# An output projection in four units of 1024 columns in place of eight of 512

## The chip, the cores and the metric

The kernel runs on one core of a Trainium2 chip. The metric is device time in microseconds (us), lower is better. The core has engines with a queue of instructions each, which run in the order of that queue and wait for each other through semaphores: PE (matrix products, with PEld loading their stationary operand), DVE (vector), ACT (scalar functions), POOL, and SP, which here only issues DMAs.

## The reference

One layer of a decoder on 256 tokens and 4096 channels, batch 1, all float32. What is computed, cut to what matters here:

```
h = rmsnorm(x, ln_g)
proj = h @ w_in                       # 256x4096 @ 4096x12288
p_x, p_gate, q, k, v, a_gate, s_u, s_gate = split(proj)
y_pool = pool_mixer(p_x)              # 1024 channels
y_attn = stick_breaking_attention(q, k, v)   # 16 heads, 2048 channels
y_ssm  = s5_mixer(s_u)                # 1024 channels, with a 1024x2048 GLU
y_* = rmsnorm(y_*, branch_g) * silu(gate of the branch)
out = rmsnorm(x + concat(y_pool, y_attn, y_ssm) @ w_out, final_g)   # 256x4096 @ 4096x4096
```

## The kernel before

Every large product is done in three passes to keep float32 accuracy: each operand is split into a rounded part `hi` and a rest `lo`, and a product is hi·hi + hi·lo + lo·hi. The activations are split once and stay on the chip as `xhl` (slots of 128 channels, with hi and lo). The weights stream in from memory in 528 pieces ("subs") of 128 partitions x 2 slots x 512 columns (512 KB). For each of them ACT writes `hi` (L232) and DVE writes `lo` (L82, the helper of all two-operand DVE work), and PE then does twelve matmuls of 512 columns: two slots, two halves of the tokens, three passes (L241 to L243). A unit is 512 output columns: 24 units of the input projection with 16 subs each, 4 GLU units with 4 subs, and 8 units of the output projection with 16 subs.

In the output projection five of a unit's sixteen subs (`SEVEN`) are done by Strassen-Winograd: the 2x2 block product of a pair of slots is formed with seven block products of 256 columns in place of eight (L189, `mm_seven`). They need sums of weight blocks (`sums_seven`, tiles `t7` and `sums7`) and of activation blocks (`sums_of_rows`, tiles `s7`), and `join_seven` puts the partial sums together once per unit.

Everything else is side work that hangs on generators, of which `pump(side_q, 3)` takes three steps per sub. The last of it is the gate of the attention branch, `att_gate` (L626): when a unit of kind `ag` has ended, its result is scaled out of PSUM (`agz`, ACT), turned into a sigmoid (`sgm`: ACT three times, DVE, ACT), multiplied with the attention output (`ao`, DVE), transposed by PE (L286, tile `ps_t`) and split into `xhl`. After the fourth `ag` unit the program calls `drain(side_q)` (L905), so this gate is written in full ahead of the first matmul of the output projection. The splits of the other 28 slots of `xhl` are written there as well (L835).

What order the engines see is decided at build time: the scheduler of the framework places PE, ACT and DVE instructions by its own simulation of when their operands are ready; SP's queue keeps the order of the program. PSUM has two pools that stay open to the end: `pmain` (two tiles of 128 x 2 x 512, in turn) for the units, and `pside` for the side work and for the sums of the seven products.

Of the kernel before, what the change touches and what calls it, by code (L numbers as in the profile page):

```python
# [2 lines left out]

# [8 lines left out]
F32 = mybir.dt.float32  # L12
# [19 lines left out]
HELD = 4  # L32
WARM = 8
SUMS_AHEAD = 1
SEVEN = (2, 5, 7, 9, 11)
# [12 lines left out]
    + [("v", V0 + 1024), ("q", Q0 + 1024), ("k", K0 + 1024)]  # L48
    + [("glu", n) for n in (1024, 0, 1536, 512)]
    + [("v", V0 + 1536), ("q", Q0 + 1536), ("k", K0 + 1536)]  # L50
# [3 lines left out]
N_SUB = 24 * 16 + 4 * 4 + 8 * 16  # L54


def body(tc, a, out, ctx):
    nc = tc.nc
    V, S, T = nc.vector, nc.scalar, nc.tensor
# [18 lines left out]
    pm = pool("pmain", space=PSUM)  # L78
    pk = pool("pside", space=PSUM)
# [13 lines left out]
    def act(o, x, f, **kw):  # L93
        S.activation(o, x, f, **kw)  # L94
# [8 lines left out]
    xt0 = bp.tile([P, 2, L], F32, tag="k4", bufs=6, name="xt")  # L103
# [3 lines left out]
    zeros = cp.tile([P, NU], BF16, name="zeros")  # L107
# [22 lines left out]
    held = []  # L130
# [8 lines left out]
    def load(i):  # L139
        w = wp.tile([P, 2, NU], F32, tag="w", bufs=LOAD_AHEAD, name="w")  # L140
        nc.sync.dma_start(w, a["ws"][i])
        wtiles[i] = w

    def hi_lo(dst_hi, dst_lo, src):
        act(dst_hi, src, AF.Copy)
        tt(dst_lo, src, dst_hi.bitcast(F32), ALU.subtract)

    def seven(i):
        return i < N_SUB and subs[i][1] in SEVEN and units[subs[i][0]][0] == "out"

    def sums_seven(i):
        w = wtiles[i]
        left, right = w[:, :, 0:L], w[:, :, L:2 * L]
        t = bp.tile([P, 4, L], F32, tag="k4", bufs=6, name="t7")
        tt(t[:, 0:2, :], right, w[:, 0, :].rearrange("p (c m) -> p c m", c=2), ALU.subtract)
        tt(t[:, 2, :], right[:, 1, :], t[:, 0, :], ALU.subtract)
        tt(t[:, 3, :], left[:, 1, :], t[:, 2, :], ALU.subtract)
        sums = bp.tile([P, 2, 4, L], F32R, tag="k8", bufs=3, name="sums7")
        hi_lo(sums[:, 0], sums[:, 1], t)
        htiles[i] = sums  # L160

    def split_seven(i):
        w = wtiles.pop(i)
        raw = []
        for kk in range(2):
            n = L if kk == 0 else NU
            hi = wp.tile([P, NU], F32R, tag="hi", bufs=5, name="hi")
            lo = wp.tile([P, NU], F32R, tag="lo", bufs=5, name="lo")
            hi_lo(hi[:, 0:n], lo[:, 0:n], w[:, kk, 0:n])
            raw.append((hi, lo))  # L170
        htiles[i] = (raw, htiles[i])

    def mm_seven(i, s, ps, pp):
        (b11, b2), sums = htiles.pop(i)
        xa, xb, y = xhl[:, 2 * s], xhl[:, 2 * s + 1], state["s7"][s]
        lo_half, hi_half = slice(0, P), slice(P, L)
        first = s == SEVEN[0]
        last = s == SEVEN[-1]
        for o, stat, mov, begin, end in (
            (pp[0], xa[:, :, lo_half], [v[:, 0:L] for v in b11], first, last),  # L180
            (ps[:, 0, 0:L], xb[:, :, lo_half], [v[:, 0:L] for v in b2], False, False),
            (ps[:, 0, L:2 * L], y[:, 2], [v[:, L:2 * L] for v in b2], False, False),
            (pp[1], y[:, 0], [sums[:, h, 0] for h in range(2)], False, last),
            (pp[3], xa[:, :, hi_half], [sums[:, h, 1] for h in range(2)], first, last),
            (pp[2], y[:, 1], [sums[:, h, 2] for h in range(2)], False, last),
            (ps[:, 1, 0:L], xb[:, :, hi_half], [sums[:, h, 3] for h in range(2)], False, False),
        ):
            for k, (p, q) in enumerate(((0, 0), (0, 1), (1, 0))):
                T.matmul(o, stat[:, p, :], mov[q], start=begin and k == 0, stop=end and k == 2, skip_group_check=True)  # L189

    def join_seven(pp, xr):
        e = bp.tile([P, 4, L], F32, tag="k4", bufs=6, name="e7")
        act(e[:, 0, :], pp[0], AF.Copy)
        tt(e[:, 3, :], e[:, 0, :], pp[2], ALU.add)
        tt(e[:, 1, :], e[:, 3, :], pp[1], ALU.add)
        tt(e[:, 2, :], e[:, 3, :], pp[3], ALU.add)
        tt(e[:, 3, :], e[:, 2, :], pp[1], ALU.add)
        tt(xr, xr, e.rearrange("p (t c) m -> p t (c m)", t=2), ALU.add)

    def sums_of_rows(qp, srcs):  # L200
        state["s7"] = {}
        for s in SEVEN:
            xa, xb = srcs(2 * s), srcs(2 * s + 1)
            t = qp.tile([P, 3, P], F32, tag="t", bufs=1, name="ts")
            tt(t[:, 0, :], xa[:, P:L], xb[:, P:L], ALU.add)
            tt(t[:, 1, :], t[:, 0, :], xa[:, 0:P], ALU.subtract)
            tt(t[:, 2, :], xb[:, 0:P], t[:, 1, :], ALU.subtract)
            tt(xa[:, P:L], xa[:, 0:P], xa[:, P:L], ALU.subtract)
            y = qp.tile([P, 3, 2, P], F32R, name="s7_%d" % s)
            hi_lo(y[:, :, 0, :], y[:, :, 1, :], t)  # L210
            state["s7"][s] = y
            yield

    def split(i):
        if seven(i):
            return split_seven(i)
        w = wtiles.pop(i)
        for kk in range(2):
            if i < KT // 2:
                split_x(2 * i + kk)  # L220
            h = 2 * (i - N_SUB + HELD) + kk
            if h < 0:
                hi = wp.tile([P, NU], F32R, tag="hi", bufs=5, name="hi")
                lo = wp.tile([P, NU], F32R, tag="lo", bufs=5, name="lo")
            elif h < 6:
                if h % 2 == 0:
                    held.append(bp.tile([P, 2, 2, NU], F32R, tag="k8", bufs=3, name="held8"))
                hi, lo = held[-1][:, kk, 0, :], held[-1][:, kk, 1, :]
            else:
                held.append(bp.tile([P, 2, NU], F32R, tag="k4", bufs=6, name="held4"))  # L230
                hi, lo = held[-1][:, 0, :], held[-1][:, 1, :]
            made = S.activation(hi, w[:, kk, :], AF.Copy)  # L232
            if i == 12:
                state["gate"] = made.ins.name
            tt(lo, w[:, kk, :], hi.bitcast(F32), ALU.subtract)
            htiles[i, kk] = (hi, lo)

    def mm_tok(ps, stat, slot, hi, lo, first, last, toks=(0, 1)):
        for t in toks:
            sl = slice(t * P, t * P + P)  # L240
            T.matmul(ps[t], stat[:, slot, 0, sl], hi, start=first, stop=False)  # L241
            T.matmul(ps[t], stat[:, slot, 0, sl], lo, start=False, stop=False)  # L242
            T.matmul(ps[t], stat[:, slot, 1, sl], hi, start=False, stop=last)  # L243


    state = {}
# [3 lines left out]
    def load_x(piece):  # L250
        xt = bp.tile([P, 2, L], F32, tag="k4", bufs=6, name="xt")
        nc.sync.dma_start(xt, a["xT"][piece])
        xtiles[piece] = xt
# [6 lines left out]
    def square_x(piece):  # L260
        xr = bp.tile([P, 2, NU], F32, tag="k4", bufs=6, name="xsq")
        nc.sync.dma_start(xr, a["xr"][piece])
        square_sums(x_sums, xr, piece)
# [17 lines left out]
    def transposed(y, kts, emit):  # L281
        for h in range(2):
# [4 lines left out]
            for c in range(2):  # L287
                emit(kts[h * 2 + c], ps[:, c * L:c * L + L])
            yield

    def keep(dst):
        def emit(kt, ps):
            act(dst(kt), ps, AF.Copy, scale=branch_g[:, kt:kt + 1])
        return emit

    def direct(kt, ps):
        slot = OUT_KT.index(kt)
        g = branch_g[:, kt:kt + 1]
        act(xhl[:, slot, 0, :], ps, AF.Copy, scale=g)
        stt(xhl[:, slot, 1, :], ps, g, xhl[:, slot, 0, :].bitcast(F32), ALU.mult, ALU.subtract)  # L300

    def square_sums(dst, y, n):
        junk = bp.tile([P, 512], BF16, tag="junk", bufs=1, name="junk")
# [20 lines left out]
    def pool_unit(u, px):  # L324
        yp = bp.tile([P, 2, NU], F32, tag="k4", bufs=6, name="ypool")
# [27 lines left out]
    ypT = bp.tile([P, 8, L], F32, tag="k8", bufs=3, name="ypT")  # L353

    def pool_gate(u, z):
        sg = bp.tile([P, 2, NU], F32, tag="k4", bufs=6, name="sgm")
# [7 lines left out]
        yield from transposed(y, [4 * u + c for c in range(4)], keep(lambda kt: ypT[:, kt, :]))  # L364


    uT = bp.tile([P, 8, L], F32, tag="k8", bufs=3, name="uT")
    glu = {}
# [109 lines left out]
    def ssm(sp, wait_u):  # L478
# [11 lines left out]
        for ct in range(8):  # L490
# [13 lines left out]
            for half in range(2):  # L504
# [13 lines left out]
                for j in range(2):  # L518
                    r0 = 32 * (2 * half + j)
                    for b in range(3):  # L520
                        side_dma(u3[32 * b:32 * b + 32, j, :], uT[r0:r0 + 32, ct, :])
# [45 lines left out]
            stt(y, uT[:, ct, :], d_skip[:, ct:ct + 1], ps[:, 0:L], ALU.mult, ALU.add)  # L567
# [4 lines left out]
            tt(uT[:, ct, :], y, l, ALU.mult)  # L572
# [6 lines left out]
    def attention(lp, g, vt, qt, kt):  # L579
        ao = lp.tile([P, 2, NU], F32, name="ao%d" % g)  # L580
        aout[g] = ao
# [41 lines left out]
        square_sums(att_sums, ao, g)  # L623
        yield
# [406 lines left out]
```

## Time and profile before

| What | us |
|---|---|
| median of 3 runs (1537.27 to 1538.69) | 1537.94 |
| the execution that was profiled, its time | 1538.15 |
| its span in the trace | 1536.4 |
| outside the span (1538.15 less 1536.4) | 1.75 |
| mean granted clock of PE | 0.998 |

The profile is one execution. A page of it gives busy times by engine, the chain of work that ended last and the costliest groups; further views give the waits, the single instructions in order of time, and busy times by stretch of the span. Times in them are counted from the start of the span. A matmul is pipelined: its row lasts longer than the step to the next one, so what a matmul costs is read from the starts of neighbours.

### The profile page before, as it was taken

Reading aid. Unit: us, or ns where it says so; the run is one execution under the profiler, and the core shown is the slowest. Engines: PE = TensorE matmul, PEld = TensorE weight load, DVE = VectorE, ACT = ScalarE, POOL = GpSimd, SP = SyncE. Lnnn points to the kernel's source line nnn. Section 1 sums busy time; section 2 is a strip of 40 time slices with the busy share of each in tenths; the row PEclk is TensorE's granted clock in tenths of the full one; section 3 lists DMA queues with packets and bytes.
Section 4 is the critical chain, followed back from the end, with each engine's and each line's share of the span. In section 5 each row is a group of like instructions: output and inputs, shape, how many; then the busy total and the mean of one; then the engine's idle time right before and its main releaser. Section 6 shows DMA issues by size and latency. Waiting matters only on the chain.

```text
span 1536.4 us, 21621 instructions
## 1 busy us (share of the span) xinstructions
PE 1521.1 (99%) x7328; PEld 1266.3 (82%) x7328; DVE 1186.9 (77%) x2304; ACT 931.6 (61%) x1677; POOL 0.2 (0%) x4
## 2 busy tenths in 40 slices
PE   9999999999999999999999999999999999999996
PEld 7888788878788888788888888888888888888885
DVE  7579878999899879897645744555677988888886
ACT  7765556766566655575546755456677655555554
POOL 0000000000000000000000000000000000000000
PEclk9999999999999999999999999999999999999999
DMA  9866655665656556554655555555655666666665
GB/s 336 310 220 202 194 179 187 196 209 185 209 187 196 189 165 200 189 179 159 191 192 178 182 185 189 192 164 178 192 183 187 218 221 213 223 210 206 216 215 199
DMA packets 94351, 308.22 MB, mean 201 GB/s; under 512 B 11808, under 2 KB 17696, under 8 KB 94240
## 3 DMA queue, kind: packets, MB, share of 16 engines
q1 hardware_dynamic: 84096, 295.92, 58.5%
q10 hardware_dynamic: 10144, 10.92, 2.5%
q8 instruction: 57, 0.93, 0.3%
q14 instruction: 54, 0.44, 0.1%
HBM read 299.45 MB, written 4.19 MB: 198 GB/s over the span
## 4 chain that ended last, share of the span: by engine, by line
PE 96%; DVE 2%; DMA 1%; ACT 0%; issue 0%; SPq 0%; DVEq 0%; ACTq 0%
PE pm L242 29%; PE pm L241 28%; PE pm L243 28%; PE ps L189 3%; PE pm L189 2%; DMA w<-in_ws 1%; PE ps_y L562 1%; PE ps_c L658 1%; DVE lo L82 1%; PE ps_bu L535 1%; PE ps_z L588 0%; PE ps_p L346 0%; PE ps_t L286 0%; DVE t L82 0%; PE ps_z L606 0%; DVE sums L82 0%
## 5 line engine op out<-in xcount | busy, mean ns | idle before, releaser
L82 DVE TENSOR_TENSOR lo<-w,hi 128x512 fp32r<-128x512 f32 (+1 forms) x1048 | 697.5, 680 | 272.5 <-ACT hi L232 266.3
L232 ACT ACTIVATE hi<-w 128x512 fp32r<-128x512 f32 x968 | 602.3, 629 | 455.0 <-PE pm L243 270.0
L242 PE MATMUL pm<-lo,xhl 128*128 128x512 f32 x1872 | 732.7, 391 | 0.2 <-DVE lo L82 0.2
L241 PE MATMUL pm<-hi,xhl 128*128 128x512 f32 x1872 | 730.9, 391 | 1.1 <-ACT xhl L94 0.6
L243 PE MATMUL pm<-hi,xhl 128*128 128x512 f32 x1872 | 731.0, 391 | 0.0
L241 PEld LDWEIGHTS pm<-hi,xhl 128*128 128x128 f32 x1872 | 351.8, 188 | 75.1 <-ACT hi L232 1.7
L242 PEld LDWEIGHTS pm<-lo,xhl 128*128 128x128 f32 x1872 | 351.8, 188 | 74.4 <-issue 2.9
L243 PEld LDWEIGHTS pm<-hi,xhl 128*128 128x128 f32 x1872 | 351.8, 188 | 71.2 <-issue 0.8
L91 DVE SCALAR_TENSOR_TENSOR et<-et,pw,tr 128x16 f32<-128x16 f32 (+3 forms) x256 | 56.2, 277 | 1.5 <-ACT tr L94 1.3
L94 ACT ACTIVATE sums<-t 128x1024 fp32r<-128x1024 f32 x40 | 42.3, 1057 | 24.6 <-DVE t L82 24.6
L82 DVE TENSOR_TENSOR sums<-t,sums 128x1024 fp32r<-128x1024 f32 x40 | 48.9, 1223 | 9.2 <-ACT sums L94 9.2
L94 ACT ACTIVATE hi<-w 128x256 fp32r<-128x256 f32 x80 | 40.0, 518 | 23.4 <-PE pm L243 19.7
L94 ACT ACTIVATE tr<-et,pw 128x32 f32<-128x32 f32 (+3 forms) x128 | 45.4, 386 | 9.6 <-DVE et L91 5.5
L189 PE MATMUL ps<-sums,s 128*128 128x256 f32 x240 | 46.8, 285 | 0.9 <-DVE sums L82 0.9
L82 DVE TENSOR_TENSOR t<-w 128x512 f32<-128x512 f32 x40 | 27.6, 690 | 22.0 <-DMA w<-in_ws 21.9
L550 DVE TENSOR_TENSOR_SCAN tb<-rho,ta 128x256 f32<-128x256 f32 x64 | 40.7, 680 | 0.1
L189 PEld LDWEIGHTS ps<-sums,s 128*128 128x128 f32 x240 | 36.7, 192 | 1.7 <-DVE sums L82 1.5
L82 DVE TENSOR_TENSOR t<-w,t 128x256 f32<-128x256 f32 x80 | 33.7, 421 | 0.3
L94 ACT ACTIVATE sgm<-sgm 128x1024 f32<-128x1024 f32 x24 | 25.3, 1052 | 0.2
L243 PE MATMUL pm<-hi,hhl 128*128 128x512 f32 x64 | 25.3, 395 | 0.0
L242 PE MATMUL pm<-lo,hhl 128*128 128x512 f32 x64 | 25.2, 393 | 0.0
L241 PE MATMUL pm<-hi,hhl 128*128 128x512 f32 x64 | 25.1, 392 | 0.0
(259 smaller groups left out, 1123.7 us busy)
## 6 DMA issues: line engine op xcount, KB each, us to landing
w<-in_ws SPq DMA_DIRECT2D x527, 512.0 KB, 3.4
xsq<-in_xr SPq DMA_DIRECT2D x8, 512.0 KB, 6.5
xr<-in_xr SPq DMA_DIRECT2D x8, 512.0 KB, 4.5
xt<-in_xT SPq DMA_DIRECT2D x15, 256.0 KB, 6.0
b<-in_bst ACTq DMA_DIRECT2D x16, 192.0 KB, 3.8
u<-uT ACTq DMA_DIRECT2D x96, 32.0 KB, 2.6
out<-o SPq DMA_DIRECT2D x6, 512.0 KB, 4.1
fg<-in_fg SPq DMA_DIRECT2D x8, 256.0 KB, 5.5
```

The costliest lines, as they stand in the source:

```text
L82: V.tensor_tensor(o, x, y, op)
L91: V.scalar_tensor_tensor(o, x, s, y, op0, op1)
L94: S.activation(o, x, f, **kw)
L189: T.matmul(o, stat[:, p, :], mov[q], start=begin and k == 0, stop=end and k == 2, skip_group_check=True)
L232: made = S.activation(hi, w[:, kk, :], AF.Copy)
L241: T.matmul(ps[t], stat[:, slot, 0, sl], hi, start=first, stop=False)
L242: T.matmul(ps[t], stat[:, slot, 0, sl], lo, start=False, stop=False)
L243: T.matmul(ps[t], stat[:, slot, 1, sl], hi, start=False, stop=last)
L535: T.matmul(ps[:, c, :], b3r[:, j, c, :], u3r[:, j, :], start=c == 0, stop=True, skip_group_check=True)
L550: V.tensor_tensor_scan(tb[:, c, :], rho[:, pr:pr + 1].broadcast_to([P, L]), ta[:, c, :], 0.0, ALU.mult, ALU.add)
L562: T.matmul(ps[32 * j:32 * j + 32, 0:L], cf[:, j, c, :], ss[j][:, c, :], start=c == 0, stop=c == 1, skip_group_check=True)
L658: T.transpose(ps[:, (c * 2 + t) * P:(c * 2 + t + 1) * P], z[:, t, (h * 2 + c) * P:(h * 2 + c + 1) * P], ident)
```

## The change

- The output projection has four units of 1024 columns. A unit still has 16 pairs of slots, but each pair comes as two subs (h = 0 and 1, one for each half of the columns, laid out so by the host).
- Six of 16 pairs are done with seven products, and a block has 512 columns. Both subs of a pair are split together (`split_seven`): four differences of 512 columns, then splits of 1024, 512, 1024 and 1024 columns.
- All other splits are of 1024 columns in one instruction per engine (before: two of 512). Rings of `hi` and `lo` hold four such splits, six in the output projection. Weight loads run six subs ahead there; for the first three units two of six land in the part of `o` that the fourth will fill.
- PSUM: the two pools are closed at the start of the output projection, and one of four tiles of two banks each is opened, of which a unit has two for its result and two for the sums of the seven products, in turn with the next unit.
- The transposed branch outputs go to DRAM (`kept`, queue of POOL), and come back during the last `ag` unit (`take_back`, queue of SP), where they are split into `xhl` four slots at a time with the row sums of their pair. So do the attention outputs (`kept_a`, read back as `ya`) and the gate of the S5 branch. `mm_tok` takes both slots for one half of the tokens before the other.
- The GLU units stand after the last v, q and k units.

What the scheduler makes of it is shown at three places. First PE's queue around the end of the last `ag` unit. Before, with `pm_11691` the tile of the first output unit, `ao3` the gated attention output, `ps_7` and `s7` of the seven products:

```order
L189 MATMUL pm_11691<-hi_11776,xhl_97 128x256
L189 MATMUL ps_7_11697<-lo_11773,xhl_97 128x256
L189 MATMUL ps_7_11697<-hi_11772,xhl_97 128x256
L189 MATMUL ps_7_11697<-sums7_11724,s7_5_11185 128x256 x3
L189 MATMUL ps_7_11697<-sums7_11724,xhl_97 128x256 x3
L189 MATMUL ps_7_11697<-sums7_11724,s7_5_11185 128x256 x3
L286 MATMUL ps_t_11663<-ident_75,ao3_9974 128x128 x4
L286 MATMUL ps_t_11672<-ident_75,ao3_9974 128x128 x4
L189 MATMUL pm_11691<-lo_11777,xhl_97 128x256
```

Now, with `pm_9715` the tile of the last `ag` unit, `pm_10130` that of the first output unit, and `ya` the gated attention output:

```order
L260 MATMUL pm_9715<-lo_10025,xhl_102 128x512
L261 MATMUL pm_9715<-hi_10024,xhl_102 128x512
L259 MATMUL pm_9715<-hi_10024,xhl_102 128x512
L260 MATMUL pm_9715<-lo_10025,xhl_102 128x512
L261 MATMUL pm_9715<-hi_10024,xhl_102 128x512
L304 MATMUL ps_t_10102<-ident_80,ya_10091 128x128 x4
L304 MATMUL ps_t_10111<-ident_80,ya_10091 128x128 x4
L259 MATMUL pm_10130<-hi_10042,xhl_102 128x512
L260 MATMUL pm_10130<-lo_10043,xhl_102 128x512
```

Before, the transposes of the last gate stood in the middle of the sixth pair of the first output unit; now they stand between the last matmul of the `ag` unit and the first of the output projection.

Second, DVE's queue from the last `agz` to the product that these transposes read. Before, the piece around the end of the gate:

```order
L91 SCALAR_TENSOR_TENSOR sgm_11654<-agz_11595,sgm_11654 128x1024
L82 TENSOR_TENSOR lo_11742<-w_11681,hi_11741 128x512
L82 TENSOR_TENSOR lo_11746<-w_11681,hi_11745 128x512
L82 TENSOR_TENSOR sums7_11724<-t7_11720,sums7_11724 128x1024
L82 TENSOR_TENSOR lo_11773<-w_11710,hi_11772 128x256
L82 TENSOR_TENSOR t7_11780<-w_11770 128x512
L82 TENSOR_TENSOR ao3_9974<-ao3_9974,sgm_11654 128x1024
```

Now (`yk` are the blocks that `take_back` brings, `ts` and `y7` their row sums, `o` the region in which a weight piece landed); ahead of this piece stand nine more rows that follow the `hi` that ACT makes between the two `agz`:

```order
L101 SCALAR_TENSOR_TENSOR sgm_10093<-agz_10088,sgm_10093 128x1024
L92 TENSOR_TENSOR ts_10048<-ts_10048,yk_10046 128x128
L92 TENSOR_TENSOR yk_10046<-yk_10046 128x128
L92 TENSOR_TENSOR t7_10176<-o_10126 128x512 x2
L92 TENSOR_TENSOR ts_10048<-yk_10046,ts_10048 128x128
L92 TENSOR_TENSOR t7_10177<-o_10126,t7_10176 128x512
L92 TENSOR_TENSOR xhl_102<-yk_10046,xhl_102 128x4x256
L101 SCALAR_TENSOR_TENSOR ya_10091<-ya_10091,r_b2048_9047,agz_10088 128x512 x2
L92 TENSOR_TENSOR t7_10177<-o_10126,t7_10177 128x512
L92 TENSOR_TENSOR lo_10185<-t7_10176,hi_10184 128x1024
L92 TENSOR_TENSOR y7_12_10052<-ts_10048,y7_12_10052 128x3x128
L92 TENSOR_TENSOR ya_10091<-ya_10091,sgm_10093 128x1024
```

The row sums and splits of the last two `yk` and the weight sums of the first seven-product pair now stand between the sigmoid and the product, ahead of the transposes.

Third, ACT's queue in the same place, now:

```order
L104 ACTIVATE agz_10088<-pm_9714,rtok_86 128x512
L104 ACTIVATE hi_10140<-w_10040 128x1024
L104 ACTIVATE agz_10088<-pm_9715,rtok_86 128x512
L104 ACTIVATE hi_10158<-w_10070 128x1024
L104 ACTIVATE sgm_10093<-agz_10088 128x1024
L104 ACTIVATE xhl_102<-yk_9998 128x4x256
L104 ACTIVATE sgm_10093<-sgm_10093 128x1024
L104 ACTIVATE y7_10_10004<-ts_10000 128x3x128
L104 ACTIVATE sgm_10093<-sgm_10093 128x1024 x2
```

Before, splits of 512 and 256 columns stood between the same steps:

```order
L94 ACTIVATE agz_11595<-pm_11206,rtok_81 128x512 x2
L94 ACTIVATE hi_11683<-w_11544 128x256
L94 ACTIVATE hi_11687<-w_11544 128x512
L94 ACTIVATE sgm_11654<-agz_11595 128x1024
L232 ACTIVATE hi_11712<-w_11573 128x512
L94 ACTIVATE sgm_11654<-sgm_11654 128x1024
```

The core of the diff:

```diff
-SEVEN = (2, 5, 7, 9, 11)
+SEVEN = (2, 4, 6, 8, 10, 12)
...
     def split_seven(i):
...
+        b, a = flat(wtiles.pop(i)), flat(wtiles.pop(i + 1))
+        b11, b21, b12, b22 = b[:, 0:NU], b[:, NU:], a[:, 0:NU], a[:, NU:]
...
+        tt(t0, b12, b11, ALU.subtract)
+        tt(t1, b22, b12, ALU.subtract)
+        raw, one, low, high = ring(), ring(), ring(), ring()
+        hi_lo(*raw, b)
+        tt(t2, b22, t0, ALU.subtract)
+        tt(t3, b21, t2, ALU.subtract)
+        hi_lo(one[0][:, 0:NU], one[1][:, 0:NU], b22)
+        hi_lo(*low, t[0])
+        hi_lo(*high, t[1])
...
+    def take_back(g):
+        t = bp.tile([P, 4, L], F32, tag="k4", bufs=K4, name="yk")
+        nc.sync.dma_start(t, kept[g])
+        for h in range(2):
+            s = 2 * g + h
+            if s in SEVEN:
+                row_sums(state["out_rows"], state["s7_out"], s, t[:, 2 * h, :], t[:, 2 * h + 1, :])
+                row_difference(t[:, 2 * h, :])
+        hi_lo(xhl[:, 4 * g:4 * g + 4, 0, :], xhl[:, 4 * g:4 * g + 4, 1, :], t)
...
     def start_end():
         nonlocal ep
         drain(side_q)
         late_ctx.close()
+        psum_ctx.close()
         ep = end_ctx.enter_context(tc.tile_pool(name="end", bufs=1, side="right", reuse_waits="tile"))
         state["o"] = ep.tile([P, 2, D], F32, name="o")
...
+        state["po"] = end_ctx.enter_context(tc.tile_pool(name="pout", bufs=1, space=PSUM, reuse_waits="tile"))
...
-            side_q.append(att_gate(lp, n, z))
-            if n == 3:
-                for i in range(28):
-                    hi_lo(xhl[:, i, 0, :], xhl[:, i, 1, :], y_src(i))
+            side_q.append(att_gate(n, z))
...
+        if kind == "ag" and c == A_G + 1536 and s >= 2 and s % 2 == 0:
+            take_back(s // 2 - 1)
...
+            mm_tok(into, rows, (2 * s, 2 * s + 1), pair, s == 0, s == nk // 2 - 1, (0,) if late else (0, 1))
...
+    sums = cp.tile([P, 2, 2], F32, name="last_sums")
     for t in range(2):
+        for h in range(2):
...
+            tt(last[:, t, cols], ps[t][:, h, :], last[:, t, cols], ALU.add)
+            act(state["joined"][t][:, h, :], last[:, t, cols], AF.Square, accum_out=sums[:, t, h:h + 1])
+        tt(out_sums[:, t, 3:4], sums[:, t, 0:1], sums[:, t, 1:2], ALU.add)
```

More of the change, by code (lines that the diff above doesn't have):

```diff
@@ L144, in hi_lo @@
     def hi_lo(dst_hi, dst_lo, src):
-        act(dst_hi, src, AF.Copy)
+        made = act(dst_hi, src, AF.Copy)
         tt(dst_lo, src, dst_hi.bitcast(F32), ALU.subtract)
-    def seven(i):
[L149 to L160, printed above, removed]
@@ new lines, in split @@
+    def split(i):
+        if i < KT // 2:
+            split_x(2 * i)
+            split_x(2 * i + 1)
+        if seven(i):
+            if subs[i][2] == 0:
+                split_seven(i)
+            return
+        w = flat(wtiles.pop(i))
+        raw = ring()
+        for n in (slice(0, NU), slice(NU, WIDE)) if i < 3 else (slice(0, WIDE),):
+            made = hi_lo(raw[0][:, n], raw[1][:, n], w[:, n])
+        if i == 12:
+            state["gate"] = made.ins.name
+        htiles[i] = raw
@@ L214, in split @@
[L214 to L236, printed above, removed]
@@ L687, in body @@
         units.append((kind, c, 8 if kind == "glu" else KT))
[L688 removed]
+    for n in range(4):
         units.append(("out", n, KT))
@@ L692, in body @@
         for s in range(nk // 2):
-            subs.append((ui, s))
+            for h in range(2 if kind == "out" else 1):
+                subs.append((ui, s, h))
     assert len(subs) == N_SUB
@@ L853, in body @@
     delayed = []
-    for i, (ui, s) in enumerate(subs):
+    for i, (ui, s, h) in enumerate(subs):
         kind, c, nk = units[ui]
```

392 lines of the change are left out of this document (203 added, 189 removed).

## The prediction

> **What bounds the kernel now.** I read the page first: how busy the engines are, and which of them the chain that ended last runs through.
>
> ```profile
> span 1536.4 us, 21621 instructions
> PE 1521.1 (99%) x7328; PEld 1266.3 (82%) x7328; DVE 1186.9 (77%) x2304; ACT 931.6 (61%) x1677; POOL 0.2 (0%) x4
> ...
> PE 96%; DVE 2%; DMA 1%; ACT 0%; issue 0%; SPq 0%; DVEq 0%; ACTq 0%
> ```
>
> PE is the bound: 96% of the chain is PE following PE. Busy PE need not be PE at its pace, so I look at PE's own waits next (engine and line, what it waited for, us in total, times, longest).
>
> ```profile
> PE ps_i L111 <- DVE zeros L108: 1.2, 1, 1.2
> PE ps L189 <- DVE sums L82: 0.9, 2, 0.5
> PE pm L241 <- DVE o L82: 0.8, 1, 0.8
> ...
> PE pm L241 <- ACT hi L232: 0.5, 1, 0.5
> ```
>
> Hardly anything: some 4 us in 1536. So time can be won only with fewer or shorter matmul steps, and is lost wherever PE is made to wait. What is a step? The timeline of PE in a quiet stretch (start, duration) gives that of 512 columns, the chain in order of time (start, length) that of 256.
>
> ```profile
> 399.82 0.39 PE L242 MATMUL pm<-lo,xhl 128*128 128x512 f32 x1
> ...
> 410.02 0.39 PE L242 MATMUL pm<-lo,xhl 128*128 128x512 f32 x1
> ```
>
> ```profile
> 1212.10 0.96 PE ps L189 x8
> ```
>
> These are the first and last of 46 rows: 45 steps in 10.20 us, 0.2267 each. Eight matmuls of 256 columns take 0.96, 0.120 each: two of them cost 0.240, six per cent more than one of 512.
>
> **Term 1, fewer and wider products: −8.3 us.** Before, a unit has 11 pairs of 12 matmuls of 512 columns and 5 pairs of 21 of 256; eight units make 1056 and 840, so 1056 x 0.2267 + 840 x 0.120 = 340.2 us. Now a unit has 10 pairs of 24 and 6 of 21, all of 512 columns; four units make 1464, and 331.9 us. The other units keep their matmuls, the side work its 456.
>
> The Trainium skill's "TensorE: Matmul & The Clock Gate", section Back-to-back issue gap, gives a warm step as the columns over 2.4 GHz plus 2.5 ns: an estimate by it is 215.8 and 109.2 ns, and a saving of 3.7 us in place of 8.3. This trace has 226.7 and 120 ns, and it decides.
>
> **Term 2, the border of input and output projection: +16 us.** The last gate's transposes are now in PE's queue ahead of the first output matmul (first place shown above). They read the product of `ya` and the sigmoid, which starts from the result of the very matmuls that end just before. Before, the same gate ran as follows (timeline of all engines; start, duration, what):
>
> ```profile
> 1179.91 1.27 ACT L94 ACTIVATE agz<-pm,rtok 128x512 f32<-128x512 f32 x2 [0.15 <-PE pm L243]
> ...
> 1181.02 1.41 DVE L91 SCALAR_TENSOR_TENSOR ao<-ao,r_b,agz 128x512 f32<-128x512 f32 x2
> ...
> 1181.90 1.05 ACT L94 ACTIVATE sgm<-agz 128x1024 f32<-128x1024 f32 x1
> ...
> 1183.37 1.06 ACT L94 ACTIVATE sgm<-sgm 128x1024 f32<-128x1024 f32 x1
> ...
> 1184.84 1.05 ACT L94 ACTIVATE sgm<-sgm 128x1024 f32<-128x1024 f32 x1
> ...
> 1188.08 1.22 DVE L91 SCALAR_TENSOR_TENSOR sgm<-agz,sgm 128x1024 f32<-128x1024 f32 x1
> ...
> 1189.47 1.04 ACT L94 ACTIVATE sgm<-sgm 128x1024 f32<-128x1024 f32 x1
> ...
> 1192.48 1.23 DVE L82 TENSOR_TENSOR ao<-ao,sgm 128x1024 f32<-128x1024 f32 x1
> ...
> 1194.71 0.49 PE L286 MATMUL ps_t<-ident,ao 128*128 128x128 f32 x3
> ```
>
> From the scaling to the transposes are 14.8 us, and PE spent them on output matmuls. In the new queue it has none that it may take. For the new length I go through DVE's queue, the later of the two, with these rows (count, busy, mean ns):
>
> ```profile
> L82 DVE TENSOR_TENSOR lo<-w,hi 128x512 fp32r<-128x512 f32 x1008 | 683.2, 690 | 272.3 <-ACT hi L232 266.3 <-ACT hi L94 0.5 <-DMA w<-in_ws 0.3
> L82 DVE TENSOR_TENSOR sums<-t,sums 128x1024 fp32r<-128x1024 f32 x40 | 48.9, 1223 | 9.2 <-ACT sums L94 9.2
> L94 ACT ACTIVATE sums<-t 128x1024 fp32r<-128x1024 f32 x40 | 42.3, 1057 | 24.6 <-DVE t L82 24.6
> ...
> L82 DVE TENSOR_TENSOR cf<-ta,tb 128x128 f32<-128x128 f32 x8 | 2.3, 287 | 0.0
> ...
> L82 DVE TENSOR_TENSOR s<-ts,s 128x384 fp32r<-128x384 f32 x5 | 2.8, 552 | 0.0
> ```
>
> Let zero be the end of the last `ag` matmul. The last five matmuls are of the other half of the tokens, so the first `agz` starts at −1.1; with 0.69 for it and 1.06 for the `hi` behind it, DVE gets its first row of this stretch at 0.65. From there to the product stand 23 rows: seven of 1024 columns (8.6), eight of 128 (2.3), two of 384 (1.1), four of 512 (2.8), and the two multiplications of `ya` (0.75 each by the row at 1181.02): 16.3 us. Neighbours overlap by some 0.09 (that row has two in 1.41), which takes off 2.0; and DVE waits some 1.1 in all for ACT, whose rows of 1.06 (sigmoid, two `yk`) come in the order shown. 0.65 + 16.3 − 2.0 + 1.1 is 16.0, which I take; 14.8 of the old one, with other rows between, is near. The bounds: the dependent steps alone are 0.69 + 4 x 1.05 + 2 x 1.22 = 7.3; with neither overlap nor early rows it is 18. While PE stands, DVE and ACT run on: four output subs (10.9 us of PE) and the sums of the first seven-product pair are then ready, so no second wait follows.
>
> **Term 3, the clock after it: +1.7 us.** A window behind PE's last work and a later one (us from and to, busy times, then PEclk), and the first matmuls of the span:
>
> ```profile
> 1525.30:1530.40 5.10, 0.00 (x0) 0.00 (x0) 3.64 (x10) 2.89 (x6) 0.00 (x0) 1.00 0.77 302
> 1530.70:1536.00 5.30, 0.00 (x0) 0.00 (x0) 0.00 (x0) 0.00 (x0) 0.00 (x0) 0.50 0.81 317
> ```
>
> ```profile
> 1.18 3.59 PE L111 MATMUL ps_i<-zeros 128*128 128x512 bf16 x8 [1.18 <-DVE zeros L108]
> ```
>
> The granted clock falls to 0.50 some 5 us after PE stops, and the first eight matmuls of 512 columns step by 0.427 (3.59 less a last one of 0.6, over 7) instead of 0.2267. A stall of 16 us passes the five. If the return takes as long as that start, 3.6 us, 8.4 steps lose 0.20 each: 1.7. Bounds 0 and 3.4 (twice as long).
>
> **Term 4, small waits that go: −0.9 us**, the wait for `sums` above: operands are ready six splits ahead now. Bounds −2 and +4: by the rows above a seven-product pair costs DVE 4 x 0.69 + 3 x 1.22 + 0.69 = 7.1 us and a plain one 2.4, a unit with join and end (4 x 0.69 + 6 x 1.22) 77 us against 83 of PE. In a window in the middle of the output projection it was 41.69 of 50:
>
> ```profile
> 1350.00:1400.00 50.00, 50.00 (x271) 43.43 (x270) 41.69 (x68) 29.27 (x52) 0.00 (x0) 1.00 0.62 207
> ```
>
> So DVE goes from 83% to 93%, still behind PE.
>
> **Term 5, the end: +0.4 us.** Before, the second half of the tokens waited for the read of the first:
>
> ```profile
> 1518.79 0.69 DVE L82 TENSOR_TENSOR o<-pm,xr 128x512 f32<-128x512 f32 x1 [1.06 <-PE pm L243]
> 1519.52 0.63 ACT L94 ACTIVATE xr<-o 128x512 f32<-128x512 f32 x1 [4.88 <-DVE o L82]
> 1519.54 0.50 PE L241 MATMUL pm<-held,xhl 128*128 128x512 f32 x1 [0.78 <-DVE o L82]
> ```
>
> Now the halves lie in tiles of their own and that 0.8 goes. But the second quarter of the last half waits for the read of the first quarter, which stands on DVE behind two additions (0.69 each), the second square on ACT (0.63) and three short rows: some 1.4. Then come an extra short addition, and one wide product (1.22) as last work where two of 512 stood. I take +0.4 (−0.8 to +1.5).
>
> **At nothing:** the wide splits of the input projection (1.22 on DVE for 1.38; a sub has 2.72 us of PE), the GLU units' new place, and the DMAs that move. Behind the seven `yk` loads on SP stand weight loads that are up to four subs, 10.9 us of PE, early; 512 KB landed in 3.4 us in the median:
>
> ```profile
> w<-in_ws SPq DMA_DIRECT2D x527, 512.0 KB, 3.4
> ```
>
> Uncovered, a late one would cost 1 or 2 us. The row sums of `take_back` fill DVE's gaps in the last `ag` unit: per two subs some 2.9 + 2.4 us against 5.44 of PE.
>
> **Sum:** the profiled execution's 1538.15 (0.21 above the median) − 8.3 + 16 + 1.7 − 0.9 + 0.4 = **1547.0 us**, 0.6% slower. What can be told from no change is about 0.2%, 3.1 us.
>
> **The rivals.**
>
> - *The gate is ready in time (faster, 1529).* If PE passed the waiting transposes, or the product stood before the last `ag` matmul ends, terms 2 and 3 fall away: 1538.15 − 8.3 − 0.9 + 0.4 = 1529.3. It decides at a stall of about 8.8 us, where term 1 is eaten up. For it: the build's scheduler took this order. Against it: the product's first operand is the `ag` result, and in the row at 1519.54 PE stood until what it waited for had come. The skill's page on TensorE calls PE's queue a partial reorder window of 64 entries that pulls weight loads ahead, and in the section The mechanism has matmuls strictly in order; by the first alone one could hope for 1529, by the second not. Chance 0.07.
> - *A short stall (same, 1537).* If DVE and ACT had done the `yk` and `t7` rows before the end of the unit, only the dependent 7.3 us would be left, too short or nearly so to touch the clock after: 1538.15 − 8.3 + 7.3 − 0.9 + 0.4 = 1536.7. Against it: these rows stand behind waits for the end of the unit. Chance 0.07.
> - *DVE takes over in the output projection (1556 or more).* At 93% any wait of DVE for a weight piece counts: the `t7` rows, which need both pieces of a pair, waited 22 us in 40 before:
>
> ```profile
> L82 DVE TENSOR_TENSOR t<-w 128x512 f32<-128x512 f32 x40 | 27.6, 690 | 22.0 <-DMA w<-in_ws 21.9
> ```
>
> At 0.55 each, 24 pairs would add 13 us to 4 x 77, still under 332; it takes 1 us per pair to pass PE, and then each further 0.4 us per pair costs 9: 1556. Chance 0.11.
>
> **How the numbers follow.** Forecast 0.75: its own range, with a stall of 10 to 18 us and the bounds of the other terms, is 1539 to 1553. The range is to leave out no more than the first rival and some of the others: 1538 to 1555. Slower: 0.75 + 0.11 = 0.86; same 0.07; faster 0.07.
>
> **What would show it.** PE's waits should list one of about 16 us for DVE `ya` at the transposes, followed by steps of 0.43 us and a dip of PEclk in the slice at 1180 us. From there to the last matmul it should be some 332 us plus the eight transposes, with steps of 0.227. If no such wait is there, term 2 is wrong and the time is near 1529; if waits for `lo` or `t7` are spread over the output units, the third rival holds.

## The result, and the profile after

| What | us |
|---|---|
| changed kernel, median of 4 runs (1548.92 to 1552.07) | 1550.53 |
| kernel before, median of 4 runs (1537.27 to 1539.75) | 1538.32 |
| ratio, 95% interval | 1.0079 (1.0061 to 1.0096) |
| profiled execution of the changed kernel, its time | 1550.40 |
| its span (before: 1536.4) | 1548.6 |

The change makes the kernel slower by 0.8%. In a later job the same kernel took 1549.06 against 1537.16 of the kernel before, ratio 1.0077 (1.0064 to 1.0091).

First the page: busy times by engine, and the row of the granted clock over the span in 40 slices.

```profile
span 1548.6 us, 19301 instructions
PE 1517.0 (98%) x6896; PEld 1243.1 (80%) x6896; DVE 1148.9 (74%) x1729; ACT 854.0 (55%) x1118; POOL 10.5 (1%) x23
...
PE   9999999999999999999999999999995999999996
...
PEclk9999999999999999999999999999998999999998
```

PE is busy for 4.1 us less than before (1517.0 against 1521.1) in a span that is 12.2 longer. One slice, the 31st, has PE at 5 tenths and the clock at 8: there the time is. PE's waits name it (engine and line, what it waited for, us in total, times, longest):

```profile
PE ps_t L304 <- DVE ya L92: 15.9, 1, 15.9
PE ps_i L121 <- DVE zeros L118: 1.2, 1, 1.2
PE pm L259 <- ACT hi L104: 0.9, 1, 0.9
PE pm L259 <- DVE o L92: 0.8, 1, 0.8
PE pm L259 <- DVE gl L92: 0.7, 1, 0.7
```

The first row is new; the one for `sums` of before is gone. The timeline of PE at the border of input and output projection (start, duration):

```profile
1180.80 0.39 PE L261 MATMUL pm<-hi,xhl 128*128 128x512 f32 x1
1197.06 1.94 PE L304 MATMUL ps_t<-ident,ya 128*128 128x128 f32 x8 [15.87 <-DVE ya L92]
1198.66 0.78 PE L259 MATMUL pm<-hi,xhl 128*128 128x512 f32 x1
1199.23 0.63 PE L260 MATMUL pm<-lo,xhl 128*128 128x512 f32 x1
1199.66 0.63 PE L261 MATMUL pm<-hi,xhl 128*128 128x512 f32 x1
...
1202.22 0.48 PE L261 MATMUL pm<-hi,xhl 128*128 128x512 f32 x1
1202.53 0.39 PE L259 MATMUL pm<-hi,xhl 128*128 128x512 f32 x1
1202.76 0.39 PE L260 MATMUL pm<-lo,xhl 128*128 128x512 f32 x1
```

The wait ends with the transposes, which then take 1.60 us to the next start; after them the starts lie 0.43 apart, and from 1202.53 on 0.227 again. In the 16 us before, DVE's and ACT's rows were these (parts of it):

```profile
1181.63 0.68 ACT L104 ACTIVATE agz<-pm,rtok 128x512 f32<-128x512 f32 x1
...
1187.48 1.22 DVE L101 SCALAR_TENSOR_TENSOR sgm<-agz,sgm 128x1024 f32<-128x1024 f32 x1
...
1189.02 1.29 DVE L92 TENSOR_TENSOR t<-o 128x512 f32<-128x512 f32 x2
...
1191.03 1.22 DVE L92 TENSOR_TENSOR xhl<-yk,xhl 128x1024 fp32r<-128x1024 f32 x1
...
1192.17 1.41 DVE L101 SCALAR_TENSOR_TENSOR ya<-ya,r_b,agz 128x512 f32<-128x512 f32 x2
...
1195.70 1.22 DVE L92 TENSOR_TENSOR ya<-ya,sgm 128x1024 f32<-128x1024 f32 x1
```

The product of the last row is what PE waits for. Between it and the sigmoid's row at 1187.48 DVE works through rows that belong to other things (`t`, `xhl<-yk`). Last, windows over the same stretch (from and to, its length, busy times of PE, PEld, DVE, ACT and POOL, then the granted clock):

```profile
1183.00:1185.00 2.00, 0.00 (x0) 0.00 (x0) 1.97 (x5) 2.00 (x3) 0.00 (x0) 1.00 1.02 408
1185.00:1187.00 2.00, 0.00 (x0) 0.00 (x0) 1.75 (x3) 2.00 (x4) 0.00 (x0) 0.58 1.03 412
1187.00:1189.00 2.00, 0.00 (x0) 0.00 (x0) 1.90 (x5) 0.71 (x2) 0.00 (x0) 0.50 0.87 346
...
1199.00:1202.40 3.40, 3.40 (x10) 2.63 (x9) 3.03 (x7) 1.34 (x3) 0.00 (x0) 0.50 0.02 5
1202.40:1206.00 3.60, 3.60 (x18) 2.96 (x17) 1.23 (x1) 1.06 (x1) 0.00 (x0) 1.00 0.00 0
```

PE stopped at 1181.03 (its last start plus one step). A window of 2 us at a mean of 0.58 that goes from 1.00 to 0.50 turns at 1185.3, 4.3 us after the stop; the clock is back at 1202.4, 5.3 us after the first transpose.

### The profile page after: what moved, and what is told of

It is laid out like the page before. It is cut to its first block, busy times and chain, and to the rows that moved or that the text cites. A ratio compares the mean times of both kernels' runs of the same rounds, so it can differ in the third digit from the quotient of the medians.

```text
span 1548.6 us, 19301 instructions
## 1 busy us (share of the span) xinstructions
PE 1517.0 (98%) x6896; PEld 1243.1 (80%) x6896; DVE 1148.9 (74%) x1729; ACT 854.0 (55%) x1118; POOL 10.5 (1%) x23
## 4 chain that ended last, share of the span: by engine, by line
PE 97%; DVE 1%; ACT 1%; DMA 0%; issue 0%; SPq 0%; DVEq 0%
PE pm L259 28%; PE pm L260 28%; PE pm L261 28%; PE p L227 4%; PE pm L227 3%; PE ps_y L599 1%; PE ps_c L693 1%; PE ps_t L304 1%; PE ps_bu L572 0%; PE ps_p L381 0%; PE ps_z L624 0%; DMA w<-in_ws 0%; PE ps_z L642 0%; PE ps_p L373 0%; PE ps_av L654 0%
## 5 line engine op out<-in xcount | busy, mean ns | idle before, releaser
L92 DVE TENSOR_TENSOR lo<-w,hi 128x1024 fp32r<-128x1024 f32 (+1 forms) x499 | 595.2, 1197 | 315.3 <-ACT hi L104 313.2
L104 ACT ACTIVATE hi<-w 128x1024 fp32r<-128x1024 f32 (+1 forms) x499 | 515.9, 1038 | 489.7 <-PE pm L261 452.0
L261 PE MATMUL pm<-hi,xhl 128*128 128x512 f32 x1856 | 725.2, 391 | 0.0
L259 PE MATMUL pm<-hi,xhl 128*128 128x512 f32 x1856 | 719.7, 391 | 2.4 <-ACT hi L104 0.9
L104 ACT ACTIVATE hi<-t 128x1024 fp32r<-128x1024 f32 x48 | 50.9, 1061 | 25.4 <-ACT hi L104 7.5
L92 DVE TENSOR_TENSOR lo<-t,hi 128x1024 fp32r<-128x1024 f32 x48 | 58.3, 1221 | 4.9 <-ACT hi L104 4.7
L104 ACT ACTIVATE hi<-o 128x1024 fp32r<-128x1024 f32 (+1 forms) x32 | 30.7, 978 | 32.5 <-PE pm L261 30.6
L92 DVE TENSOR_TENSOR lo<-o,hi 128x1024 fp32r<-128x1024 f32 (+1 forms) x32 | 35.4, 1122 | 12.0 <-ACT hi L104 11.7
L227 PE MATMUL p<-hi,y 128*128 128x512 f32 x96 | 37.6, 391 | 0.0
L227 PE MATMUL pm<-hi,xhl 128*128 128x512 f32 x96 | 37.6, 391 | 0.0
L227 PE MATMUL p<-hi,xhl 128*128 128x512 f32 x96 | 37.6, 391 | 0.0
```

The lines of the kernel that those rows point to most:

```text
L92: V.tensor_tensor(o, x, y, op)
L104: return S.activation(o, x, f, **kw)
L227: T.matmul(o, stat[:, p, :], pair[q][:, n], start=start and k == 0, stop=stop and k == 2, skip_group_check=True)
L259: T.matmul(ps[t], stat[:, slot, 0, sl], hi[:, n], start=begin, stop=False, skip_group_check=True)
L261: T.matmul(ps[t], stat[:, slot, 1, sl], hi[:, n], start=False, stop=end, skip_group_check=True)
```

## The experiments

Theory A: the change loses its gain at the border, where PE waits 15.9 us for the last gate and then runs at half clock; the output projection itself is faster, and bound by PE. Rivals: the wait costs little by itself, DVE is the bound behind it, or the wait is set by something else than DVE's queue.

**The wait alone, in the kernel before** (e3). The first output matmuls get an order dependency on the gate's transposes; nothing else changes.

```diff
-            T.matmul(ps[t], stat[:, slot, 0, sl], hi, start=first, stop=False)
+            d = T.matmul(ps[t], stat[:, slot, 0, sl], hi, start=first, stop=False)
+            if state.get("border"):
+                tc.add_manual_dep(d.ins, state["turned"], ...)
```

> The kernel before with one thing added: the first output matmuls stand behind the last gate's transposes on PE, as in the change. Theory A: PE waits from the end of the ag unit to the product, up to the 14 us that the gate took before, less where DVE and ACT get there sooner because their rings of splits are full; then half clock for some 5 us (2.6 us): slower than before by 12 to 17, 1550 to 1555. Rival B (the wait is mostly taken up again, since the splits run ahead and the waits of the output projection go): slower by less than 6, under 1544.

Measured: 1547.42, ratio 1.0059 (1.0042 to 1.0076), slower by 9.2 and short of the 12 expected. PE's timeline says why:

```profile
1180.02 0.39 PE L249 MATMUL pm<-hi,xhl 128*128 128x512 f32 x1
1182.84 0.58 PE L189 MATMUL ps<-hi,xhl 128*128 128x256 f32 x1 [2.44 <-ACT hi L94]
...
1186.26 0.84 PE L189 MATMUL ps<-sums,s 128*128 128x256 f32 x3
1191.25 1.94 PE L292 MATMUL ps_t<-ident,ao 128*128 128x128 f32 x8 [4.15 <-DVE ao L82]
1192.84 0.78 PE L241 MATMUL pm<-hi,xhl 128*128 128x512 f32 x1
```

The scheduler moved twelve products of 256 columns, which my dependency did not cover, into the gap, and the gate's product came 10.9 us after the unit's end in place of 14.0. What is left of waiting up to the transposes, 11.0 us behind the unit's end, is 9.6, the half clock is there again (starts 0.43 apart), and some small waits later go. So an old kernel with nothing of the change but the order at the border loses most of what the change loses. The rival (under 6) falls.

**Without the wait, in the changed kernel** (e1 and e2). e1 moves the seven-product pairs by two, so that their PSUM tile is free at first; e2 also leaves the last gate's transposes for the first output unit, in that tile.

```diff
-SEVEN = (2, 4, 6, 8, 10, 12)
+SEVEN = (4, 6, 8, 10, 12, 13)
```

```diff
+            if state["out"]:
+                ps = state["p7"][:, h, :]
+            else:
                 ps = pk.tile([P, 512], F32, tag="ps", bufs=2, name="ps_t")
...
+            if n == 3:
+                pump(side_q, 2)
+                state["last"] = side_q.popleft()
...
             start_end()
+            side_q.append(state["last"])
```

> The changed kernel with the seven-product pairs at 4, 6, 8, 10, 12, 13 instead of 2, 4, 6, 8, 10, 12 (still six of 16); it is also the control of e2 and e7. Theory A (PE waits at the border for the product of ya, and DVE's queue sets when that comes): the four differences of weight blocks and one of their splits (4 x 0.69 + 1.22, overlapping, 3.9 us in the trace of the change) no longer stand between the sigmoid and the product, a plain split of 1.22 does; from the trace's end of the sigmoid on DVE at 1188.7 the remaining rows take 4.4, the product ends near 1194.2 instead of 1196.9, so the wait is 13.3 us instead of 15.9 and the time 1548. Rival B (ACT's chain sets the product, DVE only fills gaps): the wait stays 15.9 and the time 1550.5.

Measured for e1: 1551.13, ratio 1.0085 (1.0070 to 1.0100). The wait for `ya` is 14.1, 1.8 shorter than in the change: DVE's rows between sigmoid and product count, though not for all of the 2.6 that I gave them. The time did not follow: the profiled execution is only 0.7 shorter than that of the change (spans 1547.9 and 1548.6), and the median is no lower. By the starts of PE the transposes begin some 2 earlier, but the end of the kernel gives back 1.5: the last wait for `o` grew from 0.8 to 1.3, and from the last matmul to the end of the span it is 12.8 us in place of 11.7. With a seven-product pair at 13, the rows that join the sums stand on DVE right before the last additions.

> e1 with the last gate's transposes put into the first output unit: they go through the PSUM tile that the unit's seven products use from pair 4 on, so PE has output matmuls to take first. Theory A (the border costs the wait of 15.9 us and 2.8 us of half clock behind it, and nothing else of the change costs as much): no long wait, no dip of the clock, 1550.5 - 15.9 - 2.8 = 1531.8, faster than before by 6.5. Rival B (DVE is short of time there: in the 16 us of the wait it was busy 14; without the wait the first output subs wait for their splits instead): waits for lo or t7 in the first eight subs of 3 us or more, 1535 or more.

Measured for e2: 1535.71, ratio 0.9984 (0.9975 to 0.9993): 15.4 us under e1, and faster than the kernel before. The long wait and the dip of the clock are gone, but 3.9 are missing from the 18.7 of theory A. PE's waits, and windows behind the border, of e2:

```profile
PE pm L260 <- DVE lo L92: 1.5, 1, 1.5
...
PE pm L259 <- DVE o L92: 0.8, 1, 0.8
```

```profile
1196.00:1201.00 5.00, 5.00 (x25) 4.12 (x25) 5.00 (x7) 0.29 (x1) 0.00 (x0) 1.00 0.61 209
1201.00:1206.00 5.00, 5.00 (x24) 4.02 (x23) 5.00 (x11) 4.14 (x7) 0.00 (x0) 1.00 0.29 110
1206.00:1211.00 5.00, 3.40 (x17) 2.19 (x15) 5.00 (x7) 2.73 (x3) 0.00 (x0) 1.00 0.47 154
```

DVE (third engine of a row) is busy without a gap for 15 us, and PE has to wait for a `lo`: rival B is right in part, with a smaller wait than its 3 us. The rows that DVE did while PE stood must still be done, and now they stand beside output matmuls. Another part of what is missing is the end, which e2 has from e1: 12.6 us behind the last matmul in place of 11.7.

**DVE in the first output unit** (e9, e12). e9 gives unit 0 only the pairs 6, 8, 10, 12. Its pairs 2 and 4 then take activation blocks whose second half has been replaced by the difference that seven products need, so unit 0 computes something else than the reference; the work of all engines is that of plain pairs.

```diff
-        return units[ui][0] == "out" and s in SEVEN
+        return units[ui][0] == "out" and s in (SEVEN if units[ui][1] else SEVEN_0)
```

> e2 with the pairs of the change (2, 4, 6, 8, 10, 12) in the output units 1 to 3 and four pairs (6, 8, 10, 12) in unit 0. In e2 PE waited 2 us for one lo at the end of pair 4's products while DVE was busy without a gap from 1196 to 1211. Theory B' (with the wait at the border gone, DVE is short in the first output unit, and that is where part of the gain went): two pairs less in unit 0 free 9 us of DVE there, the 2 us go, and 2 x 3 matmuls more cost 1.4: 1535.7 - 2.0 + 1.4 = 1535.1, with no wait of PE over 0.5 between 1181 and 1260. Rival (that wait has another cause, the gate's transposes in the PSUM tile of the products): the wait stays and the time is 1537.

Measured: 1533.97, ratio 0.9972 (0.9960 to 0.9983), with no wait of PE from 1181 to 1260 us. The wait for `lo` fits DVE's backlog: in e2's trace it is a `lo` that ends it, with DVE busy all the time before. The time alone does not settle it. e9 also moves the first use of the shared PSUM tile to pair 6, and 0.8 of the 3.0 us by which its span is shorter than e2's (1531.4 against 1534.4) lies at the end of the kernel, where the last pair is 12 again. e12 reaches the same with the full number of pairs, by another order of the pairs in unit 0:

```diff
+FIRST = (0, 1, 3, 5, 7, 9, 2, 11, 4, 6, 13, 8, 10, 12, 14, 15)
...
-                subs.append((ui, s, h))
+                subs.append((ui, FIRST[s] if (kind, c) == ("out", 0) else s, h))
...
+    wide[0] = wide[0][list(FIRST)]
```

> e2 with the six pairs of the change in every unit, and another order of the pairs in output unit 0 alone (0, 1, 3, 5, 7, 9, 2, 11, 4, 6, 13, 8, 10, 12, 14, 15), so that DVE has the border's rows behind it when the first seven-product pair comes. In e9, where the first such pair of unit 0 was also the seventh, the wait of 2 us was gone. Theory B': e9's time less the 1.4 of its two plain pairs, 1532.6, faster than before by 6 and than e2 by 3. Rival (DVE then falls behind in the denser second half of unit 0): waits for lo there of 1.5 or more, 1534 to 1536, as e2.

Measured: 1532.00 (1531.43 to 1533.58), ratio 0.9968 (0.9956 to 0.9979), **the lowest median here**, 17.1 under the changed kernel in the same job (1549.06) and 5.2 under the kernel before. Against e2 (2.5 under its own kernel before) the gain is less sure: the intervals of the two ratios just overlap. PE's waits of e12 hold nothing of the border:

```profile
PE ps_i L122 <- DVE zeros L119: 1.2, 1, 1.2
PE pm L260 <- DVE o L93: 0.8, 1, 0.8
PE pm L260 <- DVE gl L93: 0.7, 1, 0.7
PE pm L260 <- ACT xhl L105: 0.5, 1, 0.5
```

**What bounds the output projection** (e5): three seven-product pairs per unit.

```diff
-SEVEN = (2, 4, 6, 8, 10, 12)
+SEVEN = (2, 6, 10)
```

> The changed kernel with three seven-product pairs per unit (2, 6, 10) instead of six. Theory A (the output projection is bound by PE's steps): three pairs in four units gain 3 matmuls each less, so 36 matmuls of 0.229 come back: + 8.2, 1558.7; the wait at the border stays near 15.9. Rival C (DVE has become the bound of the output projection, the third rival of the prediction): DVE loses 12 x 4.7 us of work, so the time rises by less than 4 or falls.

Measured: 1556.90, ratio 1.0122 (1.0108 to 1.0135). The span is 6.4 longer than that of the change; its wait for `ya` is 1.1 shorter (14.8), and from the first transpose to the tenth output matmul it takes 4.66 us in place of 5.47, so the steps gave some 8.3, where 8.2 was expected. PE bounds the output projection; rival C falls.

**The half clock** (e6, e13, and the changed kernel again as control). Idle products fill the wait; they go to a PSUM tile that nobody reads.

```diff
+                idle = pk.tile([P, NU], F32, tag="ps", bufs=2, name="ps_i")
+                for j in range(IDLE):
+                    d = T.matmul(idle, xhl[:, 0, 0, 0:P], xhl[:, 0:2, 0, :], start=True, stop=True)
```

> The changed kernel with 60 idle products of 512 columns (13.6 us) on PE between the last ag matmul and the gate's transposes; their result is not used, and DVE's queue stands in the same order. Theory A (behind the wait, PE loses 2.8 us to a half clock, which came 4.3 us after it stopped): PE stands for some 2 us only, the clock stays at 1.00, the transposes step by 0.11 and the first matmuls by 0.227, and the end of the wait stays where it was: 1550.5 - 2.8 = 1547.7. Rival B (the lost time is that of a start behind any wait, or the idle products delay the gate): 1550.5 or more.

Measured for e6: 1550.23, ratio 1.0073 (1.0061 to 1.0086). The trace is as theory A has it:

```profile
1180.30 13.76 PE L873 MATMUL ps_i<-xhl 128*128 128x512 f32 x60
1196.35 1.07 PE L306 MATMUL ps_t<-ident,ya 128*128 128x128 f32 x8 [2.29 <-DVE ya L93]
1197.17 0.48 PE L260 MATMUL pm<-hi,xhl 128*128 128x512 f32 x1
1197.48 0.39 PE L261 MATMUL pm<-lo,xhl 128*128 128x512 f32 x1
```

From the first transpose to the start of the first output matmul it is 0.82 in place of 1.60, the next step is 0.31 in place of 0.57, and the starts behind it lie 0.23 apart. The span of this execution is 2.3 shorter than that of the change, but the median is not.

> e6 with 67 idle products (15.2 us) instead of 60. In e6's trace PE went from the first transpose to the start of the tenth output matmul in 2.97 us, against 5.47 in the trace of the change, so the half clock costs 2.5; but only the profiled one of its executions was faster, and the others had a mean clock of 0.996 against its 0.998. Theory A (there the gate came later, and the clock fell in what was left of the wait): with less of the wait left the clock is 0.998 in all of them, and the median is 2.5 under the control. Rival (the idle products cost as much as they save): the median equals the control.

> The changed kernel once more, as the control of e13 on the same chip: 1550.5.

Measured for e13: 1548.51, ratio 1.0074 (1.0061 to 1.0087); control 1549.06, 1.0077 (1.0064 to 1.0091). The mean clock was now 0.997 or 0.998 in every execution, against 0.991 to 0.994 of the control, and the profiled spans are 1545.5 and 1547.7: 2.2 shorter. The medians differ by 0.6, inside their scatter. In the control the half clock cost less than in the trace of the change (PE's timeline, then two windows, of the control):

```profile
1197.27 1.94 PE L304 MATMUL ps_t<-ident,ya 128*128 128x128 f32 x8 [15.87 <-DVE ya L92]
...
1201.65 0.39 PE L259 MATMUL pm<-hi,xhl 128*128 128x512 f32 x1
```

```profile
1185.00:1187.00 2.00, 0.00 (x0) 0.00 (x0) 1.75 (x4) 2.00 (x4) 0.00 (x0) 0.89 1.04 414
...
1199.00:1202.40 3.40, 3.40 (x14) 2.76 (x14) 3.24 (x7) 1.34 (x3) 0.00 (x0) 0.82 0.02 5
```

These are the first transpose and the tenth output matmul: 4.38 us between them, 2.98 in e13 and 5.47 in the change. The wait is the same 15.87, but the clock falls at 1186.6 and is back at 1200.2. So the half clock is shown in the traces, and cost 2.5 us in one and 1.4 in the other; that the median gains as much was not shown, and why it does not stays open.

For e6's other executions there is no trace. That the 2.3 us of wait which e6 leaves can be enough for the clock to fall is seen in e7 (below): there PE waited 2.15 us up to 1185.9, and the clock was at half from 1187.7 to 1191.1.

```profile
1187.70:1191.00 3.30, 3.30 (x9) 2.63 (x8) 0.06 (x1) 0.04 (x1) 0.00 (x0) 0.50 0.75 262
```

**Two that told little.** e7 was to shorten the wait by taking the blocks back earlier.

```diff
-        if kind == "ag" and c == A_G + 1536 and s >= 2 and s % 2 == 0:
-            take_back(s // 2 - 1)
+        if kind == "ag" and c == A_G + 1536 and s in BACK_AT:
+            take_back(BACK_AT.index(s))
```

> e1 with the seven blocks taken back at subs 2, 3, 5, 6, 8, 9, 11 of the last ag unit instead of 2, 4, ... 14, so that their row sums and splits are done before the border. Theory A: only the dependent steps are left (two scalings, four rows of ACT of 1.05, two of DVE of 1.22, one hi between): from the end of the unit to the product 8.9 us; the clock still falls, since in the trace of the change it fell 4.3 us after PE stopped, so 2.8 us of it stay: 1550.5 - 15.9 + 8.9 = 1543.5. Rival B (the short wait is too short for the clock): 1540.7. Rival C (the earlier blocks make PE wait inside the ag unit): the wait shrinks, but waits for lo of 2 us and more appear there.

Measured: 1564.18, ratio 1.0171 (1.0156 to 1.0186). The blocks overwrite slots of `xhl` from which this unit still takes `h`: its products use other data, and PE waits for the writes, 9.5 us in four waits (last unit of the input projection, PE's waits of e7):

```profile
PE pm L260 <- ACT xhl L105: 9.5, 4, 3.3
```

So theories A and B were not tested, and rival C came true in another form (waits for the writes of `xhl`, not for `lo`); the place that the change gives to the blocks is the earliest that these slots allow.

e11 took the load of the GLU bias out of e9's input projection.

```diff
-            bias = lp.tile([P, NU], F32, tag="bias", bufs=1, name="bias")
-            side_dma(bias, ...)
+            bias = biases.pop(0)
```

> e9 with the four biases of the GLU units loaded when the late pool opens, in a tile each, instead of one tile that is loaded when a unit ends. In the trace of the change DVE waited 3.7 us for the first of them and PE then 0.9 behind it, which the kernel before, with the units elsewhere, did not. Theory A: these 0.9 us go, 1534.2. Rival (PE waits there for the GLU operands anyway): no change against e9.

Measured: 1533.67, ratio 0.9970 (0.9958 to 0.9982), against 1533.97. DVE no longer waits for the bias, and PE's wait for `gl` is the same 0.7: the bias was not its cause.

## Why the prediction was right, step by step

The prediction was 1547.0 (1538 to 1555, slower); it was 1550.5. By the profiled executions, with the distances between the starts of PE's matmuls summed by stretch:

| Step of the prediction | predicted | measured |
|---|---|---|
| 1, fewer and wider products | -8.3 | -6.0 |
| 2, the wait at the border | +16 | +16.0 |
| 3, the clock after it | +1.7 | +2.6 |
| 4, small waits that go | -0.9 | -1.7 |
| 5, the end | +0.4 | 0.0 |
| at nothing: input projection | 0 | +1.3 |
| sum | +8.9 | +12.2 |

- **Term 2** carries the result, and the walk through DVE's queue gave it to 0.1 us (15.87). That it is so close is in part luck: in the trace neighbours overlap by 1.4 us in all, not 2.0, and DVE waits 0.4, not 1.1, and the two errors cancel. What made the walk possible is that the order of the queues was known before the run. PE takes its queue in order: some 1464 output matmuls stood behind eight transposes. The Trainium skill's "TensorE: Matmul & The Clock Gate", section The mechanism, has matmuls strictly in order, and the trace agrees, by this wait. The first rival (1529) fell with it, and the second, since the foreign rows did lie inside the wait; e1 moved it by moving some of them.
- **Term 3** was too small here, since it forgot the transposes: they ran at half clock too (1.60 us in place of 0.8), and the first matmul behind them took 0.57. The clock came back 5.3 us after the first transpose, not 3.6. But its size changes from run to run: in the repetition, with the same wait, the clock came back after 3.0 us and the loss was 1.1 smaller. So a close number would have been luck as well. The Trainium skill's "TensorE: Matmul & The Clock Gate", section What's actually happening, gives a window of some 3.4 us that runs free of the kernel, and has the clock fall after one idle window or more. The window is in these traces (last section); the full idle window is not, since in e3 the clock fell 2.3 us after PE stopped, and that measurement decides.
- **Term 1** had the count right and the step too short. I took 0.2267 from a quiet stretch; in the changed output projection a step is 0.229 on average. Before, the distances of the output matmuls sum to 1.3 us more than the steps of the prediction (0.2267 and 0.120), now to 3.6 more. (The side work has 632 matmuls in both traces, not 456; that changes nothing in the sum.)
- **Term 4**: the waits for `sums` were 1.7 in all by the starts, and they went.
- **Cost at nothing**: the input projection lost 1.3. Some 0.9 of it is PE's wait for `gl` where the GLU units now follow the last attention unit; its cause is open (not the bias, by e11).
- **The range** was wide enough, but its inner part was not added up as said: the bounds of all terms in full reach from 1537 to 1557, not from 1539 to 1553.
- **The third rival** fell: DVE was busy for 249.95 of the 300 us from 1200 to 1500, 83% and not 93%; the estimate had added durations that overlap, as its own note on neighbours says. It came true only where the prediction did not look, in the first output unit once the wait is gone (e2, e9).

The sum of six windows of 50 us, in the same order of columns:

```profile
sum 300.00, PE 300.00 PEld 245.31 DVE 249.95 ACT 162.80 POOL 0.00; mean PE 50.00 PEld 40.89 DVE 41.66 ACT 27.13 POOL 0.00
```

## What to carry to other kernels

Read the order of the engines' queues at each border of stages before arguing about costs: closing a pool, or draining side work ahead of a stage, can put a late result's consumer ahead of work that could run (which of the two did it here was not tried apart), and an in-order engine then pays the whole chain, and the clock after it. A wait that long also hides what the other engines do meanwhile; when it is removed, this work needs a place, and here the best time came after the heavy pairs of the first unit were put later. A gain of 0.4% in matmul steps is real, and is lost by one such border.

## What the runs showed of the hardware

The clock turns on a grid of its own. The stretch at half clock lasted 17.07 us in the change (1185.34 to 1202.40), 13.65 in the control (the changed kernel once more), in e1, e3 and e5, and 3.41 three times in e7: five, four and one times 3.41. Where the grid lies against the wait differs between the traces. The clock fell 4.3 us after PE's stop in the change, 5.3 in the control and 2.3 in e3, and came back 5.3, 3.0 and 4.9 us after the first transpose. So the same wait has more than one price.

The step of the same matmul of 512 columns differs with the place of its split in the ring of six, in the same way in all units of the trace of the change, of its repetition and of e5, where the pairs lie elsewhere. Counted from 0 as `ring` counts, a plain sub steps by 0.2267 in places 1, 2 and 3, by 0.2283 in place 0, and by 0.2333 in places 4 and 5, the two whose tiles lie in the pool that the output projection opens. Two neighbouring subs on PE's timeline:

```profile
1370.60 0.39 PE L259 MATMUL pm<-hi,xhl 128*128 128x512 f32 x1
...
1373.32 0.39 PE L259 MATMUL pm<-hi,xhl 128*128 128x512 f32 x1
...
1376.12 0.39 PE L259 MATMUL pm<-hi,xhl 128*128 128x512 f32 x1
```

Twelve steps from the first to the second row take 2.72 us, twelve from the second to the third 2.80, with no wait in either and the clock at 1.00. The place is not all of it: in the input projection all four places of its ring stepped by 0.2267 for long stretches, and so did place 0 in the first sub that used it, behind the wait (1205.96 to 1208.68). The output projection pays some 2 us more for it than before. What else it takes was not tried, and stays open.
